# FFN input products in two token halves of 256 columns, with the activations moved by 320 bytes

## The chip, the core and the metric

The kernel runs on one core of a Trainium2 chip. The metric is the device time of one execution in microseconds, the median of several runs. The engines are PE (TensorE, matmuls, with its weight loads listed apart as PEld), DVE (VectorE), ACT (ScalarE), POOL (GpSimd) and SP (which here issues DMAs).

## The reference

One decoder layer for 512 tokens of width 1024 in float32. What matters here is its last part:

```
h = layer_norm(ALPHA * h + mixed @ w_out, ln1_g, ln1_b)
a, u = split(h @ w_ffn_in, 2)            # 1024 -> 2 x 2816
a = causal_dwconv(a, conv_w, conv_b)     # width 3, along the tokens
f = (gelu(a) * u) @ w_ffn_out            # 2816 -> 1024
out = layer_norm(ALPHA * h + f, ln2_g, ln2_b)
```

Ahead of it stand an input projection, a block-sparse attention branch, a pooling branch and their gated merge; the change does not touch them.

## The kernel before, in words

Every large product is made of three matmuls in a rounded 32-bit format (`fp32r`): both operands are split into a high part and a low part, and high x high, high x low and low x high are summed in PSUM. `mm3` (L144 to L148) issues the three; so nearly all matmuls of the profile stand on the lines L146, L147 and L148, and are told apart by the tile that they write (`fi` is the FFN input). A matmul holds one operand (128 x 128, loaded by LDWEIGHTS) and streams the other one past it, up to 512 columns.

The FFN input stage works feature-major. The activations after the first layer norm are transposed on PE (`ln1_T`, L537) into `hT_hi` and `hT_lo`, each 128 partitions x 8 k-tiles x 512 tokens of 4 bytes; a k-tile's row of 512 tokens is 2,048 bytes. They are the streamed operand. The weights `w_ffn_in` come in 44 chunks of 128 x 1024, gate and value columns alternating. `fetch` (L92) loads a chunk by a DMA on SP, ACT copies the high part (`whi`, L67) and DVE subtracts the low part (`wlo`, L68); there are three raw buffers and a ring of five split ones (`RING` = 5), and `weights(i)` (L139) asks for chunks up to three ahead. A buffer of the ring comes free when the last matmul that reads it is done.

`fi_mm(j, b, t)` (L575) computes chunk j for the tokens `t` into the PSUM bank `b`: 8 k-tiles x 3 matmuls. The first five chunks run in two passes of 256 tokens, the first 256 tokens of all five ahead of the others (L618 to L629), because the transposes of the last two token tiles (`ln1_T(2)` and `ln1_T(3)`) are still to be done in between. The other 39 chunks (L632 to L642) run with 512 columns at once. After every second chunk `gated` (L580) applies the convolution, GELU and the product with the value half on ACT and DVE, and `formed` (L607) prepares operands of the FFN output, which follows at L703 with products `foe`, `foa`, `fob`, `fod` and `fo_cut`.

The order on each engine is that of the program as a scheduler lays it out at build time. Tiles are placed in SBUF by pools in the order of their opening: `hTp` (L464) opens behind `ypool` and holds `hT_hi` and `hT_lo` alone, and the pool `fp` takes its place after the stage. With 16,384 bytes each, `hT_hi` begins at byte 101,056 of its partition and `hT_lo` at 117,440.

Of the kernel before, what the change touches and what calls it, by code (L numbers as in the profile page):

```python
# [8 lines left out]
F32 = mybir.dt.float32  # L9
# [5 lines left out]
P = 128  # L15
S = 512
D = 1024
KT = D // P
# [25 lines left out]
def layer_kernel(ctx: ExitStack, tc: tile.TileContext, xT, x, w_v, w_c, rel_bias, invcnt, w_group,  # L44
# [11 lines left out]
    def bank(name):  # L56
        return ps.tile([P, S], F32, tag="ps", name=name)
# [56 lines left out]
    def half(name, sl):  # L114
        return w_fo[int(name[1]) - 1, 2 - int(name[2])][:, sl]

    def piece(c):
        return slice(c * D, min((c + 1) * D, KH * S))
# [20 lines left out]
    def weights(i):  # L139
        while state["next"] <= min(i + LEAD, state["limit"]):  # L140
            fetch()
        return ready[i]

    def mm3(out_, w, a, start, stop, **kw):  # L144
        (wh, wl), (ah, al) = w, a
        nc.tensor.matmul(out_, wh, ah, start=start, stop=False, **kw)  # L146
        nc.tensor.matmul(out_, wh, al, start=False, stop=False, **kw)  # L147
        nc.tensor.matmul(out_, wl, ah, start=False, stop=stop, **kw)  # L148

    def split3(v, a):  # L150
        return tuple(t.rearrange("p (a c) -> p a c", a=a) for t in v)
# [83 lines left out]
    for kt in range(KT):  # L235
        wh, wl = split3(weights(kt // 2), 2)
        wh, wl = wh[:, kt % 2, :], wl[:, kt % 2, :]
# [189 lines left out]
    for f in range(KT):  # L427
        if f == KT - LEAD:
            state["limit"] = WO0 + RING - 1
        wh, wl = split3(weights(BR0 + f), KT)  # L430
# [4 lines left out]
        for br in (1, 0):  # L435
            b = bank(f"br{f}_{br}")
# [3 lines left out]
            t = bp.tile([P, S], F32, tag="m", name=f"m{f}_{br}", bufs=4)  # L440
# [21 lines left out]
    ytiles = [ypool.tile([P, S], F32, name=f"y{j}") for j in range(2)]  # L462
    hp = ExitStack()
    hTp = hp.enter_context(tc.tile_pool(name="hTp", bufs=1, reuse_waits="tile"))  # L464
    hT_hi = hTp.tile([P, KT, S], F32R, name="hT_hi")
    hT_lo = hTp.tile([P, KT, S], F32R, name="hT_lo")
    st = const.tile([P, NT, 4, 6], F32, name="st")
# [69 lines left out]
    def ln1_T(i):  # L537
        for n in range(2):
            b = bank(f"ht{i}_{n}")
            for k in range(4):  # L540
                kt = 4 * n + k
                nc.tensor.transpose(b[:, k * P:(k + 1) * P], xs[:, i, kt * P:(kt + 1) * P], ident)
            split(hT_hi[:, 4 * n:4 * n + 4, i * P:(i + 1) * P], hT_lo[:, 4 * n:4 * n + 4, i * P:(i + 1) * P],
                  b.rearrange("p (a c) -> p a c", a=4))
# [29 lines left out]

    def fi_mm(j, b, t):  # L575
        wh, wl = split3(weights(FI0 + j), KT)
        for kt in range(KT):
            mm3(b[:, t], (wh[:, kt, :], wl[:, kt, :]), (hT_hi[:, kt, t], hT_lo[:, kt, t]), kt == 0, kt == KT - 1)

    def gated(j, a, u):  # L580
        y = ytiles[j % 2]
        nc.scalar.activation(y, a, AF.Identity, bias=cvp[:, j, 3:4], scale=cvp[:, j, 2:3])
        nc.vector.scalar_tensor_tensor(y[:, 1:], a[:, :S - 1], cvp[:, j, 1:2], y[:, 1:], op0=ALU.mult, op1=ALU.add)
        nc.vector.scalar_tensor_tensor(y[:, 2:], a[:, :S - 2], cvp[:, j, 0:1], y[:, 2:], op0=ALU.mult, op1=ALU.add)  # L584
        nc.scalar.activation(y, y, AF.Gelu)  # L585
        nc.vector.tensor_tensor(fT[:, j, :], y, u, op=ALU.mult)  # L586
# [9 lines left out]
    t1, t2 = slice(0, 256), slice(256, 512)  # L596
# [10 lines left out]
    def formed(j):  # L607
        for c in cuts:
            if j == c.stop - 1:
                nc.vector.tensor_tensor(rd(c), side(0, c, t1), side(0, c, t2), op=ALU.subtract)  # L610
                side_split(0, c, rd(c))
            if j == KH + c.stop - 1:
                nc.vector.tensor_tensor(side(0, c, t2), side(1, c, t2), side(0, c, t2), op=ALU.subtract)
                nc.vector.scalar_tensor_tensor(rd(c), side(1, c, t2), -1.0, rd(c),
                                               op0=ALU.mult, op1=ALU.subtract)

    hb = {}
    for j in range(RING):  # L618
        hb[j] = bank(f"fi{j}")
        fi_mm(j, hb[j], slice(0, 256))  # L620
        if j == 0:
            ln1_T(2)
        elif j == RING - 2:
            ln1_T(3)
    for j in range(RING):
        state["limit"] = FI0 + RING + j
        fi_mm(j, hb[j], slice(256, 512))
        if j % 2:
            gated(j // 2, hb[j - 1], hb[j])  # L629
    state["limit"] = len(chunks) - 1  # L630
    ra = hw.tile([P, 8, 256], F32, tag="lnb", name="ra")
    for j in range(RING, 2 * NF):  # L632
        hb[j] = bank(f"fi{j}")
        fi_mm(j, hb[j], slice(0, S))
        if j % 2:
            f = j // 2
            gated(f, hb[j - 1], hb[j])
            formed(f)
            if f % 2 == 0 and f >= 6 and f < 6 + 2 * NC:
                c = f // 2 - 3  # L640
                nc.sync.dma_start(tw[:, piece(c)], half("B22", piece(c)))
                nc.gpsimd.dma_start(tw[:, piece(c)], half("B12", piece(c)), accum_op=ALU.add)  # L642
# [166 lines left out]
```

## Time and profile before

| what | value |
|---|---|
| median of 3 runs | 660.53 us (659.76 to 660.55) |
| the profiled execution: its own time | 659.63 us |
| its span, first to last instruction | 657.8 us |
| granted TensorE clock, mean | 0.996 |
| PE busy | 647.0 us |
| DVE / ACT / POOL busy | 384.9 / 284.7 / 95.5 us |

The profile is taken from one execution; the 1.8 us between its time and its span lie ahead of the first and behind the last instruction. Its views used here are: the page with the busy time of each engine and the chain of work that ended last; the groups of instructions by line, engine and shape, with count, total and mean; the timeline, one row for each instruction with its start and its length in us; the stretches, with the busy time of each engine in each; and the waits, which name the engine that waited, for whom, for how long in total, how often, and the longest. A matmul's end in the records is modelled, and matmuls overlap; what one costs in a gapless row is the distance from its start to the next one's.

### The profile page before, as it was taken

The page shows a single profiled execution, that of the slowest core. Times are in us where ns is not written, and L with a number is a line of the kernel's source. Part 1 is how long each engine was busy: PE and PEld are TensorE (multiplying, and loading weights), DVE is VectorE, ACT ScalarE, POOL GpSimd, SP SyncE. Part 2 cuts the span into 40 slices and gives each one's busy share as a digit, 9 for nine tenths or more (in the row PEclk, how much of TensorE's full clock was granted, in tenths as well). Part 3 has the DMA queues.
Part 4 walks back from the last instruction along what each step waited for, and adds up shares of the span by engine and source line. Part 5 has one row for each costly group of instructions (what it writes and reads, how often), then busy time and mean ns, then how long its engine had stood idle before and what let it go on. Part 6 is the DMA issues. An engine that isn't in the chain of part 4 may idle for free.

```text
span 657.8 us, 8016 instructions
## 1 busy us (share of the span) xinstructions
PE 647.0 (98%) x3082; PEld 537.6 (82%) x3082; DVE 384.9 (59%) x560; ACT 284.7 (43%) x393; POOL 95.5 (15%) x139
## 2 busy tenths in 40 slices
PE   8999999999999999999999999999999999999994
PEld 6888787877888888889988888888888888888884
DVE  6466665554532675398455344444534548789596
ACT  6547547585422233132443333333333336555452
POOL 1615351111000124102100000000000001123302
PEclk9999999999999999999999999999999999999998
DMA  8643222212222228209942222232222334979905
GB/s 319 213 145 97 81 83 77 97 64 70 92 96 97 96 97 305 79 1 302 255 146 97 97 96 97 96 99 99 95 96 100 96 99 107 219 180 190 283 4 128
DMA packets 24918, 83.70 MB, mean 127 GB/s; under 512 B 3240, under 2 KB 3496, under 8 KB 24624
## 3 DMA queue, kind: packets, MB, share of 16 engines
q1 hardware_dynamic: 19024, 63.24, 27.6%
q0 software_dynamic: 5280, 18.90, 13.3%
q10 hardware_dynamic: 576, 1.05, 0.5%
q8 instruction: 24, 0.39, 0.2%
q14 instruction: 14, 0.11, 0.1%
HBM read 80.01 MB, written 3.17 MB: 126 GB/s over the span
## 4 chain that ended last, share of the span: by engine, by line
PE 94%; DVE 2%; POOL 2%; ACT 1%; DMA 1%; issue 0%; DVEq 0%; ACTq 0%; POOLq 0%
PE fi L148 12%; PE fi L147 12%; PE fi L146 12%; PE g L146 4%; PE g L148 4%; PE g L147 4%; PE v L247 3%; PE wo L147 2%; PE br L148 2%; PE br L147 2%; PE wo L148 2%; PE wo L146 2%; PE br L146 2%; PE fod L148 2%; PE foa L148 2%; PE foa L147 2%
## 5 line engine op out<-in xcount | busy, mean ns | idle before, releaser
L68 DVE TENSOR_TENSOR wlo<-wraw,whi 128x1024 fp32r<-128x1024 f32 (+1 forms) x105 | 134.6, 1286 | 116.0 <-ACT whi L67 114.2
L67 ACT ACTIVATE whi<-wraw 128x1024 fp32r<-128x1024 f32 (+1 forms) x104 | 108.8, 1048 | 183.7 <-PE fi L147 83.6
L147 PE MATMUL fi<-hT_lo,whi 128*128 128x512 f32 (+1 forms) x392 | 143.8, 367 | 0.0
L148 PE MATMUL fi<-hT_hi,wlo 128*128 128x512 f32 (+1 forms) x392 | 143.8, 367 | 0.0
L146 PE MATMUL fi<-hT_hi,whi 128*128 128x512 f32 (+1 forms) x392 | 143.5, 368 | 0.0
L147 PEld LDWEIGHTS fi<-hT_lo,whi 128*128 128x128 f32 x392 | 73.9, 189 | 12.2
L148 PEld LDWEIGHTS fi<-hT_hi,wlo 128*128 128x128 f32 x392 | 73.9, 189 | 12.1
L146 PEld LDWEIGHTS fi<-hT_hi,whi 128*128 128x128 f32 x392 | 73.6, 189 | 12.1
L134 POOL DMA_DIRECT2D tw<-in_w_fo x18 | 15.8, 913 | 267.2 <-DVE wlo L68 267.2
L146 PE MATMUL g<-xT_hi,whi 128*128 128x512 f32 x128 | 50.3, 393 | 0.0
L148 PE MATMUL g<-xT_hi,wlo 128*128 128x512 f32 x128 | 49.9, 390 | 0.0
L147 PE MATMUL g<-xT_lo,whi 128*128 128x512 f32 x128 | 49.8, 389 | 0.0
L67 ACT ACTIVATE whi<-tw 128x1024 fp32r<-128x1024 f32 (+1 forms) x30 | 29.5, 985 | 25.0 <-PE fi L147 11.3
L586 DVE TENSOR_TENSOR fT<-y,fi 128x512 f32<-128x512 f32 x22 | 15.1, 688 | 40.3 <-PE fi L148 39.6
L68 DVE TENSOR_TENSOR wlo<-tw,whi 128x1024 fp32r<-128x1024 f32 (+1 forms) x30 | 33.4, 1131 | 8.4 <-ACT whi L67 8.3
L585 ACT ACTIVATE y<-y 128x512 f32<-128x512 f32 x22 | 13.9, 633 | 43.1 <-DVE y L584 43.1
L148 PEld LDWEIGHTS g<-xT_hi,wlo 128*128 128x128 f32 x128 | 24.0, 188 | 5.1
L146 PEld LDWEIGHTS g<-xT_hi,whi 128*128 128x128 f32 x128 | 24.0, 188 | 5.0 <-issue 0.2
L147 PEld LDWEIGHTS g<-xT_lo,whi 128*128 128x128 f32 x128 | 24.1, 188 | 4.9
L352 POOL TENSOR_SCALAR pp<-pp,rs 128x128 f32<-128x128 f32 (+3 forms) x32 | 21.8, 698 | 37.5 <-PE g L148 18.3
L444 POOL TENSOR_TENSOR mt<-m,m 128x512 f32<-128x512 f32 x8 | 11.2, 1394 | 96.0 <-DVE m L441 79.3
L146 PE MATMUL wo<-whi,mx_hi 128*128 128x512 f32 x64 | 25.0, 390 | 0.0
(204 smaller groups left out, 1185.6 us busy)
## 6 DMA issues: line engine op xcount, KB each, us to landing
wraw<-in_w_fi SPq DMA_DIRECT2D x44, 512.0 KB, 3.3
wraw<-in_w_c SPq DMA_DIRECT2D x28, 512.0 KB, 3.3
tw<-in_w_fo POOLq DMA_DIRECT2D x20, 512.0 KB, 7.3
tw<-in_w_fo SPq DMA_DIRECT2D x10, 512.0 KB, 3.6
wraw<-in_w_fo SPq DMA_DIRECT2D x10, 512.0 KB, 3.5
wraw<-in_w_br SPq DMA_DIRECT2D x8, 512.0 KB, 3.2
wraw<-in_w_out SPq DMA_DIRECT2D x8, 512.0 KB, 3.2
strip<-F_d POOLq DMA_DIRECT2D x8, 256.0 KB, 3.6
```

Source lines behind the costliest of these rows:

```text
L67: nc.scalar.activation(hi, src, AF.Copy)
L68: nc.vector.tensor_tensor(lo, src, hi.bitcast(F32), op=ALU.subtract)
L134: nc.gpsimd.dma_start(raw, half(then[1:], sl), accum_op=ALU.add)
L146: nc.tensor.matmul(out_, wh, ah, start=start, stop=False, **kw)
L147: nc.tensor.matmul(out_, wh, al, start=False, stop=False, **kw)
L148: nc.tensor.matmul(out_, wl, ah, start=False, stop=stop, **kw)
L247: nc.tensor.matmul(bs[j], xs_[j][a], (wh, wl)[b], start=kt == 0 and n == 0, stop=False)
L352: nc.gpsimd.tensor_scalar(pp[:, offs[i]:offs[i] + n], pp[:, offs[i]:offs[i] + n], rs[:, i:i + 1], 1.0, op0=ALU.mult, op1=ALU.mult)
L444: nc.gpsimd.tensor_tensor(mt, m[1], m[0], op=ALU.add)
L585: nc.scalar.activation(y, y, AF.Gelu)
L586: nc.vector.tensor_tensor(fT[:, j, :], y, u, op=ALU.mult)
```

## The change

An unused tile of 80 floats (320 bytes in each partition) is placed ahead of `hT_hi` in its pool, so that `hT_hi` begins at byte 101,376 and `hT_lo` at 117,760. `fi_mm` takes a tuple of token ranges and runs all k-tiles for one range after the other; the first five chunks pass one range of 256 tokens at a time, as before, and the 39 others pass both, so that each 512-column matmul becomes two of 256 columns with a weight load each. `t1` and `t2` are the slices 0:256 and 256:512 (L596).

```
+    hTp.tile([P, 80], F32, name="hT_gap")
     hT_hi = hTp.tile([P, KT, S], F32R, name="hT_hi")
     hT_lo = hTp.tile([P, KT, S], F32R, name="hT_lo")
...
     def fi_mm(j, b, t):
         wh, wl = split3(weights(FI0 + j), KT)
-        for kt in range(KT):
-            mm3(b[:, t], (wh[:, kt, :], wl[:, kt, :]), (hT_hi[:, kt, t], hT_lo[:, kt, t]), kt == 0, kt == KT - 1)
+        for c in t:
+            for kt in range(KT):
+                mm3(b[:, c], (wh[:, kt, :], wl[:, kt, :]), (hT_hi[:, kt, c], hT_lo[:, kt, c]), kt == 0, kt == KT - 1)
...
     for j in range(RING):
         hb[j] = bank(f"fi{j}")
-        fi_mm(j, hb[j], slice(0, 256))
+        fi_mm(j, hb[j], (t1,))
...
     for j in range(RING):
         state["limit"] = FI0 + RING + j
-        fi_mm(j, hb[j], slice(256, 512))
+        fi_mm(j, hb[j], (t2,))
...
     for j in range(RING, 2 * NF):
         hb[j] = bank(f"fi{j}")
-        fi_mm(j, hb[j], slice(0, S))
+        fi_mm(j, hb[j], (t1, t2))
```

More of the change, by code (lines that the diff above doesn't have):

```diff
@@ L464, in layer_kernel @@
     hTp = hp.enter_context(tc.tile_pool(name="hTp", bufs=1, reuse_waits="tile"))
+    hTp.tile([P, 80], F32, name="hT_gap")
     hT_hi = hTp.tile([P, KT, S], F32R, name="hT_hi")
@@ L576, in fi_mm @@
         wh, wl = split3(weights(FI0 + j), KT)
-        for kt in range(KT):
-            mm3(b[:, t], (wh[:, kt, :], wl[:, kt, :]), (hT_hi[:, kt, t], hT_lo[:, kt, t]), kt == 0, kt == KT - 1)
+        for c in t:
+            for kt in range(KT):
+                mm3(b[:, c], (wh[:, kt, :], wl[:, kt, :]), (hT_hi[:, kt, c], hT_lo[:, kt, c]), kt == 0, kt == KT - 1)
     def gated(j, a, u):
@@ L619, in layer_kernel @@
         hb[j] = bank(f"fi{j}")
-        fi_mm(j, hb[j], slice(0, 256))
+        fi_mm(j, hb[j], (t1,))
         if j == 0:
@@ L626, in layer_kernel @@
         state["limit"] = FI0 + RING + j
-        fi_mm(j, hb[j], slice(256, 512))
+        fi_mm(j, hb[j], (t2,))
         if j % 2:
@@ L633, in layer_kernel @@
         hb[j] = bank(f"fi{j}")
-        fi_mm(j, hb[j], slice(0, S))
+        fi_mm(j, hb[j], (t1, t2))
         if j % 2:
```

## The prediction

> **What bounds the kernel now.** I read the page's head first, then the stretches of the kernel, then the matmuls one by one.
>
> ```profile
> span 657.8 us, 8016 instructions
> PE 647.0 (98%) x3082; PEld 537.6 (82%) x3082; DVE 384.9 (59%) x560; ACT 284.7 (43%) x393; POOL 95.5 (15%) x139
> PE 94%; DVE 2%; POOL 2%; ACT 1%; DMA 1%; issue 0%; DVEq 0%; ACTq 0%; POOLq 0%
> ```
>
> PE is busy for 98% of the span, and 94% of the chain that ended last is PE's. A busy row is not yet a bound, because matmuls overlap; so the next view is the busy time of each engine in the stretches before the FFN input, in its first part (halves of 256 columns), in its main part (512 columns) and behind it.
>
> ```profile
> 301.20:331.50 30.30, 30.30 (x256) 30.28 (x255) 17.14 (x29) 10.87 (x15) 5.34 (x6) 1.00 1.00 287
> 331.50:543.90 212.40, 212.40 (x940) 175.97 (x939) 101.63 (x110) 70.93 (x85) 0.00 (x0) 1.00 0.29 100
> ```
>
> The columns are length, then PE, PEld, DVE, ACT, POOL busy with counts, the granted clock, DMA share and GB/s. In the main part PE has no idle time in 212.4 us, while DVE works 102 us and ACT 71 us. The clock is 1.00 in both. What this stage costs is therefore the number of matmuls times the distance from one start to the next. The grouped view, shapes apart, gives the counts:
>
> ```profile
> L146 PE MATMUL fi<-hT_hi,whi 128*128 128x512 f32 x312 | 121.4, 389 | 0.0
> L146 PE MATMUL fi<-hT_hi,whi 128*128 128x256 f32 x80 | 22.1, 285 | 0.0
> ```
>
> The same counts stand on L147 and L148, so 936 matmuls of 512 columns and 240 of 256. Their means (389 and 285 ns) are from start to modelled end, and they overlap; the price of one is the distance of starts, read from the timeline. Two stretches of it, the first with 512-column and 256-column forms next to each other:
>
> ```profile
> 300.99 0.39 PE L148 MATMUL wo<-whi,mx_lo 128*128 128x512 f32 x1
> 301.22 0.28 PE L146 MATMUL fi<-hT_hi,whi 128*128 128x256 f32 x1
> 301.33 0.28 PE L147 MATMUL fi<-hT_lo,whi 128*128 128x256 f32 x1
> 301.45 0.28 PE L148 MATMUL fi<-hT_hi,wlo 128*128 128x256 f32 x1
> ...
> 303.97 0.28 PE L148 MATMUL fi<-hT_hi,wlo 128*128 128x256 f32 x1
> ```
>
> ```profile
> 331.74 0.40 PE L146 MATMUL fi<-hT_hi,whi 128*128 128x512 f32 x1
> 331.97 0.40 PE L147 MATMUL fi<-hT_lo,whi 128*128 128x512 f32 x1
> ...
> 543.70 0.39 PE L148 MATMUL fi<-hT_hi,wlo 128*128 128x512 f32 x1
> 543.92 0.39 PE L146 MATMUL foe<-whi,sd_hi 128*128 128x512 f32 x1
> ```
>
> From 331.74 to 543.70 there are 935 steps: 211.96 us / 935 = **226.7 ns for 512 columns**. From 301.33 to 303.97 there are 22 steps: 2.64 us / 22 = **120.0 ns for 256 columns**. The difference, 106.7 ns for 256 columns, is 0.4167 ns for each column; so 512 columns take 213.3 ns and a rest of **13.3 ns** is left, and 256 columns take 106.7 ns with the same rest of 13.3 ns. In these two rows the rest does not depend on the length: it is paid for each matmul.
>
> **The change part by part.**
>
> *Two halves in place of one.* The main part has 44 - 5 = 39 chunks of weights, each with 8 k-tiles and 3 products: 936 matmuls, as counted above. Each becomes two of 256 columns, with its own weight load: PE has 936 matmuls and 936 loads more. By the rows, a pair costs 2 x 120.0 = 240.0 ns in place of 226.7, that is +13.3 ns; 936 x 13.3 ns = **+12.5 us**. All of it is on the path, since PE has no idle time here. A chunk's 24 products grow from 5.44 to 5.76 us.
>
> *The loads of weights.* The weight-load rows say whether they still hide:
>
> ```profile
> 305.08 0.19 PEld L148 LDWEIGHTS fi<-hT_hi,wlo 128*128 128x128 f32 x1
> 305.20 0.19 PEld L146 LDWEIGHTS fi<-hT_hi,whi 128*128 128x128 f32 x1
> 305.32 0.19 PEld L147 LDWEIGHTS fi<-hT_lo,whi 128*128 128x128 f32 x1
> ```
>
> In the halves they follow each other each 120 ns too, 0.19 us long, so two are in flight, and PEld is busy for 30.28 of 30.30 us against 175.97 of 212.40 in the main part. Their cost is inside the 120.0 ns, which I therefore don't add to. PE's stream of instructions doubles in rate, but the 240 matmuls of the halves already run at that rate for 30 us without a gap.
>
> *The order inside a chunk.* All k-tiles of the first half now come before those of the second. The last matmul of a chunk still ends both halves of the bank, so the gating on ACT and DVE, the ring of five weight buffers and the next stage are released by the same instruction as before. In the built programs the lists of ACT, DVE, POOL and SP, waits included, are the same; only PE's differs, by the 936. What waits in the main part waits for PE:
>
> ```profile
> ACT whi L67 <- PE fi L147: 95.0, 39, 4.4
> DVE fT L586 <- PE fi L148: 37.6, 19, 2.3
> SPq L108 <- DVE wlo L68: 159.2, 33, 7.2
> ...
> L68 DVE TENSOR_TENSOR wlo<-wraw,whi 128x1024 fp32r<-128x1024 f32 x36 | 44.1, 1224 | 63.4 <-ACT whi L67 62.2
> L67 ACT ACTIVATE whi<-wraw 128x1024 fp32r<-128x1024 f32 x36 | 38.3, 1063 | 85.9 <-PE fi L147 83.6 <-DMA wraw<-in_w_fi 2.3
> ```
>
> ACT waits 39 times for PE, to be given a buffer back, 95.0 us in total: weights are ready ahead, and a slower PE gives these engines more room. I cost this at nothing; the cover would be gone only with chunks shorter than the 2.29 us of copy and subtraction (1,063 and 1,224 ns), far below 5.4 us. Behind the stage, the FFN output begins one step after the last input matmul (543.70, 543.92) and moves as a whole.
>
> *The 320 bytes.* The empty tile has no instruction. Its only effect is the address of the activations: as the pools lay them out, hT_hi begins at byte 101,056 of its partition before (98 x 1024 + 704) and at 101,376 = 99 x 1024 after, hT_lo 16,384 further on; each half of a row (1,024 bytes) then begins on a multiple of 1,024. The weights, at 704 bytes past such a multiple plus steps of 512, don't move. What the address is worth no row shows: in this kernel every operand of this number type that PE streams begins 64 bytes past a multiple of 128 (704 or 960 past one of 1,024), and the distance is 226.7 ns in the input projections, the branch and output products and the FFN alike. I bound it from both sides. The best case is that the whole rest of 13.3 ns goes in all 2 x 936 + 240 = 2112 matmuls of the stage: 2112 x 13.3 = -28.2 us, against the +12.5. The worst, by the same size with the other sign, is +28.2 us. I take 0: a constant cost for each matmul needs no further cause to explain both rows.
>
> By the Trainium skill, page "SBUF — State Buffer", section Specifications, the memory has lines of 16 bytes, and a crossing into a new one is what costs. By that the edit is worth nothing, for 101,056 and 101,376 are both multiples of 16, and the forecast stays at +12.5 us; no run here shows it.
>
> The sum is made against the profiled execution, 659.63 us (span 657.8): 659.6 + 12.5 = 672.1. The median of the runs shown, 660.53, stands 0.9 above it, and I give a value between the two bases: **672.6 us**.
>
> **The rivals.**
>
> *The rest of 13.3 ns is a matter of the address (ends faster).* If PE fetches its stream in lines of 128 bytes, 32 columns of 4 bytes each, then 2,048 bytes that begin 64 past a line touch 17 lines and 1,024 bytes touch 9: 17 x 32 x 0.4167 = 226.7 ns and 9 x 32 x 0.4167 = 120.0 ns. That fits both rows as well as the constant does. At the new address it would be 8 lines, 106.7 ns: a pair 213.3 in place of 226.7 (936 x -13.3 = -12.5 us), and the 240 of the first part 13.3 ns less each (-3.2): 659.6 - 15.7 = 643.9. Against it: a load of weights goes with each matmul, its address is unchanged, and PEld is gapless in the halves, so a load may set the 120.0 ns there by itself; then nothing is won. The one shorter step of that part is the first (301.22 to 301.33, 0.11 us), whose load had been done under a long matmul. So the gain may stop at some 113 ns, where a pair costs 226 (936 x -0.7 = -0.6, 240 x -7 = -1.7: 657.3 us). The rival decides for faster wherever the new distance is under 114.1 ns (2112 x d = 936 x 226.7 + 240 x 120.0). Its time: between 643.9 and 657.3, at 109.5 ns, in the middle, 659.6 - 2112 x 4.6 ns = 649.9 us.
>
> The Trainium skill, page "TensorE: Matmul & The Clock Gate", section Back-to-back issue gap, gives columns / 2.4 + 2.5 ns for one warm matmul. By it a split would cost an estimated 936 x 2.5 = 2.3 us; at the old address the trace disagrees (120.0 ns against 109.2), and at the new one 109.2 ns would give an estimated -10.4 us. Its section on LDWEIGHTS gives columns / 1.2, 107 ns for 128, which would let the rival have nearly all of its gain.
>
> *The two nearly cancel (no change).* The distance falls to 113.5 to 114.7 ns: within 1.3 us of before, by the same equation.
>
> *The new address is worse.* The stream and the weights now begin at different places within 128 bytes (0 and 64), where before both were at 64. If that costs up to another 13.3 ns each, the time is up to 672.1 + 28.2 = 700.3. For it speaks only that no such pair is in the trace.
>
> **How the numbers follow.** A measurement of this kernel tells about 0.2% (1.3 us) from no change. Forecast, 671.5 to 673.5: 0.54. Slower, but with part of the rest gone (662 to 671): 0.04. Slower still: 0.02. Rival with the address: 0.35. Cancelled: 0.05. So slower 0.60, same 0.05, faster 0.35. The likeliest case's own range is 671.5 to 673.5; the range that is to hold 8 in 10 must reach into the faster rival, most of whose room lies above 646, so it goes from 646 to 674.
>
> **What would show it.** In the changed profile, the fi group of 512 columns is gone and that of 256 counts 2112. Distance of starts at 120.0 ns: the stage from 331.7 lasts 936 x 240.0 = 224.6 us in place of 212.2, and the first part stays at 30.5 us; the forecast holds. At 107 to 113 ns in both parts: the address mattered, and the first part, which is not split, would shrink by 1.7 to 3.2 us; this alone tells address from split. Above 120 ns: the new address is bad. The forecast would also be wrong if ACT or DVE became late, which would show as PE idle time before L146.

## The result and the profile after

The changed kernel takes 667.78 us (median of 4 runs, 667.68 to 669.95) against 660.54 us (4 runs, 659.76 to 660.57): ratio 1.012, 95% interval 1.0099 to 1.0142. It is slower by 7.2 us. The forecast was 672.6 us and slower, that is 12.1 us over this median of before (12.5 by its sum). The sign holds; the size came out smaller.

The head of the changed kernel's page, and its chain:

```profile
span 668.2 us, 9888 instructions
PE 657.4 (98%) x4018; PEld 583.5 (87%) x4018; DVE 385.0 (58%) x560; ACT 283.9 (42%) x393; POOL 93.1 (14%) x139
PE 93%; DVE 2%; POOL 2%; ACT 1%; DMA 0%; issue 0%; DVEq 0%; ACTq 0%; POOLq 0%
```

PE has 936 instructions and 936 weight loads more, DVE, ACT and POOL have as many as before, and the chain is still PE's. The stretches, with the columns as in the prediction, cut near the borders of the stage's parts (the first row begins 2.4 us ahead of the first FFN matmul, so it still holds some matmuls of the product before):

```profile
301.20:333.60 32.40, 32.40 (x268) 31.97 (x267) 19.07 (x31) 11.78 (x15) 5.33 (x6) 1.00 1.00 286
333.60:554.08 220.48, 220.48 (x1874) 220.48 (x1873) 101.64 (x110) 70.94 (x84) 0.00 (x0) 1.00 0.30 97
```

PE is gapless, the clock is 1.00, and in the main part PEld is now gapless too (220.48 of 220.48 us). The waits behind PE in the main part grew with it, as they should where PE sets the pace:

```profile
ACT whi L67 <- PE fi L147: 102.2, 38, 4.6
DVE fT L588 <- PE fi L148: 39.4, 19, 2.4
```

So again only the distance of starts counts. The groups and the timeline of the changed kernel, from the first matmul of the stage over the first of its main part to the first behind it:

```profile
L146 PE MATMUL fi<-hT_hi,whi 128*128 128x256 f32 x704 | 196.0, 279 | 0.0
```

```profile
303.58 0.28 PE L146 MATMUL fi<-hT_hi,whi 128*128 128x256 f32 x1
...
333.61 0.28 PE L146 MATMUL fi<-hT_hi,whi 128*128 128x256 f32 x1
...
553.97 0.28 PE L148 MATMUL fi<-hT_hi,wlo 128*128 128x256 f32 x1
554.09 0.39 PE L146 MATMUL foe<-whi,sd_hi 128*128 128x512 f32 x1
```

The main part takes 554.09 - 333.61 = 220.48 us for 1872 matmuls, **117.8 ns each** and not 120.0; a pair is 235.6 ns against 226.7. That is 936 x 8.9 ns = +8.3 us (220.48 against 212.19). The first part, which is not split, takes 30.0 us against 30.5: its 240 matmuls became about 2 ns shorter too. The sum is +7.8 us, and the medians say +7.2. This one profiled execution (669.95 us) is about 2.2 us above the other three of the kernel. In its trace the first FFN matmul starts 2.4 us later than in the trace of before (303.58 against 301.22), and the lag is there already at the first matmul of the input projections (29.18 against 26.74), ahead of everything that the change touches; the other three left no trace, so that this is their whole difference is likely and not shown.

The address was thus worth something, which I had put at nothing. The question for the experiments is what.

### The profile page after: what moved, and what is told of

It reads as the page before. It is cut to its first block, busy times and chain, and to the rows that moved or that the text cites. A ratio compares the mean times of both kernels' runs of the same rounds, so it can differ in the third digit from the quotient of the medians.

```text
span 668.2 us, 9888 instructions
## 1 busy us (share of the span) xinstructions
PE 657.4 (98%) x4018; PEld 583.5 (87%) x4018; DVE 385.0 (58%) x560; ACT 283.9 (42%) x393; POOL 93.1 (14%) x139
## 4 chain that ended last, share of the span: by engine, by line
PE 93%; DVE 2%; POOL 2%; ACT 1%; DMA 0%; issue 0%; DVEq 0%; ACTq 0%; POOLq 0%
PE fi L147 13%; PE fi L146 12%; PE fi L148 12%; PE g L146 4%; PE g L148 4%; PE g L147 4%; PE v L247 3%; PE wo L148 2%; PE br L148 2%; PE br L146 2%; PE wo L146 2%; PE wo L147 2%; PE br L147 2%; PE fod L147 2%; PE fod L146 1%; PE foa L147 1%
## 5 line engine op out<-in xcount | busy, mean ns | idle before, releaser
L147 PE MATMUL fi<-hT_lo,whi 128*128 128x256 f32 x704 | 196.9, 280 | 0.0
L148 PE MATMUL fi<-hT_hi,wlo 128*128 128x256 f32 x704 | 196.3, 279 | 0.0
L146 PE MATMUL fi<-hT_hi,whi 128*128 128x256 f32 x704 | 196.0, 279 | 0.0
L147 PEld LDWEIGHTS fi<-hT_lo,whi 128*128 128x128 f32 x704 | 132.2, 188 | 0.0
L146 PEld LDWEIGHTS fi<-hT_hi,whi 128*128 128x128 f32 x704 | 132.0, 188 | 0.0
L148 PEld LDWEIGHTS fi<-hT_hi,wlo 128*128 128x128 f32 x704 | 131.7, 187 | 0.0
L146 PE MATMUL g<-xT_hi,whi 128*128 128x512 f32 x128 | 50.3, 393 | 0.0
L148 PE MATMUL g<-xT_hi,wlo 128*128 128x512 f32 x128 | 49.9, 390 | 0.0
L147 PE MATMUL g<-xT_lo,whi 128*128 128x512 f32 x128 | 49.8, 389 | 0.0
L68 DVE TENSOR_TENSOR wlo<-tw,whi 128x1024 fp32r<-128x1024 f32 (+1 forms) x30 | 33.3, 1129 | 9.0 <-ACT whi L67 9.0
L148 PEld LDWEIGHTS g<-xT_hi,wlo 128*128 128x128 f32 x128 | 24.0, 188 | 5.1
L146 PEld LDWEIGHTS g<-xT_hi,whi 128*128 128x128 f32 x128 | 24.0, 188 | 5.0 <-issue 0.2
L147 PEld LDWEIGHTS g<-xT_lo,whi 128*128 128x128 f32 x128 | 24.0, 188 | 4.9
L146 PE MATMUL wo<-whi,mx_hi 128*128 128x512 f32 x64 | 25.0, 390 | 0.0
L148 PE MATMUL wo<-whi,mx_lo 128*128 128x512 f32 x64 | 24.9, 389 | 0.0
```

The source lines that it names most:

```text
L68: nc.vector.tensor_tensor(lo, src, hi.bitcast(F32), op=ALU.subtract)
```

## The experiments

All times are medians beside runs of the kernel before on the same chip (660.2 to 660.5 us); the distances of starts are from the traces. My theory was that PE fetches its stream in lines of 128 bytes, and that weight loads then set a floor of 117.8 ns. The rival was a small gain from the address for any matmul.

**The 320 bytes alone** (39 chunks at 512 columns):

```
+    hTp.tile([P, 80], F32, name="hT_gap")
     hT_hi = hTp.tile([P, KT, S], F32R, name="hT_hi")
```

> The kernel before with the empty 320 bytes alone; the 39 chunks stay at 512 columns. Line theory (a matmul streams its operand in lines of 128 bytes, so a start 64 bytes past a line costs one line, 13.3 ns; the 117.8 ns of the split kernel is then a floor set by the weight loads): 512 columns fall from 226.7 to between 213.3 and 216 ns, 936 x -13.3 to -10.7 ns, and the 240 short ones to 117.8 (-0.5 us): 647.5 to 650.0 us. Rival, small-address theory (the rest of 13.3 ns is constant, and the address takes 2.25 ns off each matmul of either length): 936 x -2.25 and 240 x -2.25 ns, 657.9 us.

Measured: 661.97 us, ratio 1.0024 (1.0014 to 1.0034). Both theories fall: it is slower. The timeline of this kernel, its first FFN matmul, the borders of the main part and four matmuls inside it:

```profile
301.83 0.28 PE L146 MATMUL fi<-hT_hi,whi 128*128 128x256 f32 x1
...
331.86 0.40 PE L146 MATMUL fi<-hT_hi,whi 128*128 128x512 f32 x1
...
399.85 0.39 PE L146 MATMUL fi<-hT_hi,whi 128*128 128x512 f32 x1
400.08 0.39 PE L147 MATMUL fi<-hT_lo,whi 128*128 128x512 f32 x1
400.31 0.39 PE L148 MATMUL fi<-hT_hi,wlo 128*128 128x512 f32 x1
400.54 0.39 PE L146 MATMUL fi<-hT_hi,whi 128*128 128x512 f32 x1
...
546.11 0.40 PE L146 MATMUL foe<-whi,sd_hi 128*128 128x512 f32 x1
```

214.25 us / 936 = **228.9 ns**: 2.2 ns more for 512 columns, at the same address that takes 2.2 ns off 256 columns (the first part, 301.83 to 331.86, is 30.0 us here too).

**The split alone**:

```
-    hTp.tile([P, 80], F32, name="hT_gap")
```

(taken out of the changed kernel)

> The split alone, activations at the old address. Both theories: 240.0 ns for a pair in place of 226.7, 936 x 13.3 ns = +12.5 us: 673.0 us. If it comes out at 667.8 as with the gap, the long run of short matmuls and not the address made 117.8 ns of 120.0.

Measured: 672.26 us, ratio 1.0175 (1.0158 to 1.0192). The timeline, borders of the main part:

```profile
331.60 0.28 PE L146 MATMUL fi<-hT_hi,whi 128*128 128x256 f32 x1
...
556.24 0.40 PE L146 MATMUL foe<-whi,sd_hi 128*128 128x512 f32 x1
```

224.64 us / 1872 = 120.0 ns. The split costs what the prediction worked out, +12.45 us in the trace; the 117.8 ns is the address's doing.

**64 bytes in place of 320** (`hTp.tile([P, 16], F32, name="hT_gap")`, unsplit):

> The kernel before with an empty 64 bytes in place of 320, unsplit: the activations begin on a multiple of 128 and 256 bytes, 768 past one of 1024. Line theory: as with 320 bytes, 647.5 to 650.0 us. Small-address theory: 657.9 if a multiple of 128 is enough, 660.5 if it needs a multiple of 512 or 1024.

Measured: 662.28 us, ratio 1.0024 (1.0014 to 1.0034), with 228.9 ns and a first part of 30.0 us. The same as 320 bytes: a start on a multiple of 1,024 is not what counts.

**The weights moved along** (one empty tile ahead of the weight pool moves everything behind it, the activations included):

```
+    const.tile([P, 80], F32, name="gap")
     wp = ctx.enter_context(tc.tile_pool(name="wp", bufs=1))
```

> The 320 bytes laid ahead of the weight buffers, so that weights and activations both begin on multiples of 1024; unsplit. The split weights are streamed in the token-major products (v 96, attention-and-merge output 192, FFN output 429 of 512 columns and 66 of 256). Line theory: the FFN input as with the gap alone, and 783 matmuls more of up to -13.3 ns (-10.4 us): 637 to 641 us. Small-address theory: (1176 + 783) x -2.25 ns = -4.4, 656.1 us. If what matters is that streamed and held operand begin at different places within 128 bytes, nothing changes: 660.5 us.

Measured: 664.65 us, ratio 1.0052 (1.0037 to 1.0067). The rows of this kernel: the FFN input's main part, then 42 steps of the gate projections ahead of it:

```profile
336.36 0.40 PE L147 MATMUL fi<-hT_hi,whi 128*128 128x512 f32 x1
...
548.55 0.39 PE L147 MATMUL foe<-whi,sd_hi 128*128 128x512 f32 x1
```

```profile
195.62 0.39 PE L147 MATMUL g<-xT_hi,whi 128*128 128x512 f32 x1
...
205.43 0.39 PE L147 MATMUL g<-xT_hi,whi 128*128 128x512 f32 x1
```

The FFN input is back at 212.19 / 936 = 226.7 ns, though its activations lie where they lay in the run with the gap alone: **not the address of the stream counts, but its place relative to that of the weights**. And the gate projections, whose stream stayed while the weights moved, went from 226.7 to 9.81 us / 42 = 233.6 ns (233.3 over the 214 steps without a gap around them). With 672 such matmuls in the input projections (28 tiles x 24), 672 x 6.6 ns = 4.4 us is the most that they can lose; from the starts of their matmuls they lose about 3.3 us, since not all of them stood in gapless rows. The output product ahead of the FFN (0.4 us) and the FFN output (0.5 us) make up the rest of the 4.2 us by which the median lies above before.

The FFN output tells the same with the roles exchanged: there the weights stream and the activations are held. Its product `fob` has in this run all its streamed starts 64 bytes behind the held ones, counted within 256:

```profile
578.62 0.39 PE L147 MATMUL fob<-whi,sd_hi 128*128 128x512 f32 x1
...
593.50 0.39 PE L149 MATMUL fob<-whi,sd_lo 128*128 128x512 f32 x1
```

14.88 us / 65 = 228.9 ns, the figure of the FFN input with the gap alone; before, the same 65 steps took 226.7 ns each.

Compare the two cases of a stream that lies elsewhere than the weights: the FFN input with the gap alone (228.9 ns) and the gate projections here (233.3 ns). Taken within 128 bytes, they are the same pair of places exchanged; within 256 bytes the streamed start lies 64 behind the weights in the first and 192 in the second. The next runs ask for the period.

**32 and 96 bytes, and the weights at the other place** (gap tiles of 8 and of 24 floats; `const.tile([P, 16], ...)` with a gap of 16):

> The kernel before with an empty 32 bytes ahead of the activations, unsplit: streamed starts 96 past a multiple of 128, weights still at 64. Relation theory (what counts is where the streamed start lies to the start of the weights within 128 bytes; equal gives 226.7 and 120.0 ns for 512 and 256 columns, streamed 0 and weights 64 gives 228.9 and 117.8, streamed 64 and weights 0 gives 233): a new distance, 512 columns between 226.7 and 233 ns, 660.5 to 666.4 us. Rival, granules of 64 bytes (only the 64-byte block of the start counts): 96 is in the block of 64, nothing changes, 660.5 us.

> The kernel before with an empty 96 bytes, unsplit: streamed starts 32 past a multiple of 128, weights at 64. Relation theory: a distance other than that at 0, 512 columns between 224 and 233 ns, 658 to 666 us. Granules of 64 bytes: 32 is in the block of 0, 228.9 and 117.8 ns as with 64 or 320 bytes, 662.1 us.

> 64 bytes ahead of the weight buffers and 64 more ahead of the activations, unsplit: weights at 0 and activations at 64 past a multiple of 128, the reverse of the changed kernel. Relation theory: 512 columns at 233 ns as in the input projections of the run with the weights alone moved against their stream, 256 columns other than 117.8 by the same sum; the other stages as in that run (664.7), the FFN input 936 x 6.3 ns more: 670.5 us. Rival, the streamed address alone counts: the FFN input is back at 226.7 and 120.0 ns, 664.7 us.

Measured: 665.85 us (ratio 1.0084, 1.0064 to 1.0104), 666.62 us (1.0086, 1.0053 to 1.0119) and 665.57 us (1.0075, 1.0055 to 1.0095). The main part is 218.40 us in the first two, 233.3 ns for a matmul, and 214.25 us in the third, 228.9 ns. Blocks of 64 bytes are out. The third kernel's borders of the main part:

```profile
337.76 0.40 PE L147 MATMUL fi<-hT_hi,whi 128*128 128x512 f32 x1
...
552.01 0.39 PE L147 MATMUL foe<-whi,sd_hi 128*128 128x512 f32 x1
```

In the third I had counted within 128 bytes and expected 233; within 256 the stream lies 64 behind the weights, as in the run with the gap alone, and takes the same 228.9.

**128, 192 and 224 bytes**, gap tiles of 32, 48 and 56 floats:

> The kernel before with an empty 128 bytes, unsplit: the streamed starts lie 128 bytes behind those of the weights, counted within 256. If the relation repeats every 128 bytes, this is the same as no gap: 226.7 and 120.0 ns, 660.5 us. Rival, it repeats every 256 (so the input projections, 192 apart after the weights alone were moved, take 233.2 ns, and the FFN input, 64 apart, 228.9): a distance not yet seen, above 226.7 ns for 512 columns, 661 to 667 us.

> The kernel before with an empty 192 bytes, unsplit. If the relation repeats every 256 bytes, the FFN input takes the 233.2 ns that the input projections took when 192 bytes lay between their two starts: 936 x 6.5 ns = +6.1 us, 666.6 us. Rival, it repeats every 128 bytes: as with 64 or 320 bytes, 228.9 ns, 662.1 us.

> The kernel before with an empty 224 bytes, unsplit. If the relation repeats every 128 bytes, this is the case of 96 bytes: 233.3 and 119.7 ns, 666.6 us. Rival, every 256 bytes: a place not yet seen, between 226.7 and 237 ns for 512 columns, 660.5 to 670 us; below 226.7 only if some place other than 0 is the best one.

Measured: 666.04 us (ratio 1.0094, 1.0074 to 1.0113), 666.06 us (1.0088, 1.0068 to 1.0108) and 666.88 us (1.0100, 1.0076 to 1.0124). The kernel with 128 bytes, borders of its main part:

```profile
331.76 0.40 PE L146 MATMUL fi<-hT_hi,whi 128*128 128x512 f32 x1
...
550.16 0.39 PE L146 MATMUL foe<-whi,sd_hi 128*128 128x512 f32 x1
```

218.40 us / 936 = 233.3 ns; the other two have the same. The period is not 128 bytes, and the 192 bytes foretold from the gate projections came out.

**256 bytes**, a gap tile of 64 floats:

> The kernel before with an empty 256 bytes, unsplit. If only the distance of the two starts within 256 bytes counts, the move is none: 226.7 and 120.0 ns, 660.2 us as before. Rival, any move away from the old place costs, or the relation has a longer period: 228.9 to 233.3 ns for 512 columns, 662 to 666.5 us.

Measured: 660.39 us, ratio 1.0005 (0.9992 to 1.0018): no change, by a move of 256 bytes. Its main part:

```profile
333.85 0.40 PE L146 MATMUL fi<-hT_hi,whi 128*128 128x512 f32 x1
...
546.04 0.39 PE L146 MATMUL foe<-whi,sd_hi 128*128 128x512 f32 x1
```

212.19 us / 936 = 226.7 ns. At the two places tried both ways, 0 and 64 (a gap of 64 and one of 320 bytes), the relation repeats every 256 bytes. In one table, for the FFN input. The 512 columns are the main part divided by 936. The 256 columns are the mean of the 236 steps without a gap in the first part; at 0 it is the main part of the split alone, and the first parts there give 119.9:

| streamed start behind the weights' start, within 256 bytes | 512 columns | 256 columns |
|---|---|---|
| 0 (before, split alone, both moved, gap 256) | 226.7 ns | 120.0 ns |
| 32 | 233.3 | 116.7 |
| 64 (the change, gap 64, gap 320, weights at 0) | 228.9 | 117.8 |
| 96 | 233.3 | 120.0 |
| 128 | 233.3 | 118.8 |
| 192 | 233.3 | 117.8 |
| 224 | 233.3 | 118.3 |

**Half a load.** Does the weight load take part, or only the two addresses?

```
-            mm3(b[:, t], (wh[:, kt, :], wl[:, kt, :]), (hT_hi[:, kt, t], hT_lo[:, kt, t]), kt == 0, kt == KT - 1)
+            nc.tensor.matmul(b[:, t], wh[:, kt, :], hT_hi[:, kt, t], start=kt == 0, stop=False)
+            nc.tensor.matmul(b[:64, t], wh[:, kt, :64], hT_lo[:, kt, t], start=False, stop=False)
+            nc.tensor.matmul(b[:, t], wl[:, kt, :], hT_hi[:, kt, t], start=False, stop=kt == KT - 1)
```

> The kernel before, but the second of the three products of the FFN input (high weights x low activations) holds only 64 of the 128 weight columns, so half of that small correction is left out and that load is half as long. If the rest of 13.3 ns comes from the reads of the load (128 columns of it against the stream), it halves for one matmul in three, whichever the length: 392 x -6.7 ns = -2.6 us, 657.9 us. If the rest belongs to the matmul itself or to the change of weights, nothing changes: 660.5 us.

Measured: 662.20 us, ratio 1.0024 (1.0012 to 1.0035). The loads of this kernel, and the borders of its main part:

```profile
399.98 0.14 PEld L579 LDWEIGHTS fi<-hT_lo,whi 128*64 128x64 f32 x1
400.22 0.19 PEld L580 LDWEIGHTS fi<-hT_hi,wlo 128*128 128x128 f32 x1
400.45 0.19 PEld L578 LDWEIGHTS fi<-hT_hi,whi 128*128 128x128 f32 x1
```

```profile
331.74 0.39 PE L578 MATMUL fi<-hT_hi,whi 128*128 128x512 f32 x1
...
546.82 0.39 PE L146 MATMUL foe<-whi,sd_hi 128*128 128x512 f32 x1
```

Neither number came: with the same addresses and streams, one shorter load in three (0.14 us in place of 0.19) moves the 512-column distance up, 215.08 us / 936 = 229.8 ns, and the 256-column one down, to 116.9 ns. That the load takes part in what a matmul costs, the runs with the weights moved had shown by its address. This run adds that it is not so many reads that are simply added. Whether the load's length does it is not shown: with 64 weight columns the matmul also writes 64 partitions in place of 128, and the run can't tell the two apart.

## Why the prediction was right in sign and off in size

- *PE's distances of starts bound the stage, and what waits, waits for PE.* Held: no idle time on PE before or after, nothing late behind it.
- *The split costs 936 x 13.3 ns = +12.5 us.* Held, shown alone: 120.0 ns, +12.45 us in the trace, +11.8 us in the medians.
- *The loads are inside the 120.0 ns, the new order in a chunk costs nothing.* Held for the sum.
- *The 320 bytes: "I take 0".* This is the term of the sum that was mis-sized. It is worth 2112 matmuls x -2.2 ns = -4.7 us in the split kernel, inside the bounds of -28.2 to +28.2. The reason I gave for 0, a constant cost for each matmul, is false: the rest depends on where the streamed start lies relative to the weights' start within 256 bytes. In the kernel before, all pairs that I had compared lay at the same place, 0, which is why one constant fitted them. I had set the two addresses against each other only in the last rival, within 128 bytes and for a loss alone.
- *The rival of the 128-byte lines* was right that the address matters and had the mechanism wrong: as run later, it foretold a gain for 512 columns too, which lose 2.2 ns. Its test, a first part that shrinks by 1.7 to 3.2 us, showed 0.5 us. Its point of decision, 114.1 ns, was sound: 117.8 lies above it, and the change is slower.
- *The rival "the new address is worse"*, from streamed and held operand at different places: it named the right relation with the wrong sign. The changed kernel's matmuls have 256 columns, and they gain 2.2 ns; 512 columns, which it no longer has there, lose 2.2 ns at this place and up to 6.6 at others.
- The 16-byte rule of the Trainium skill, page "SBUF — State Buffer", section Specifications, for which I said that no run shows it: by it the gap alone would be worth nothing. The runs disagree, 226.7 to 228.9 ns with a start that is a multiple of 16 both times.
- *The range.* The measured 667.78 us lies outside the 671.5 to 673.5 of the likeliest case. It is the case "slower, but with part of the rest gone (662 to 671)", which I gave a chance of 0.04. The range of 646 to 674 holds it because it was stretched down to a faster rival that did not come; that is luck. The sign is not: the split's +12.5 us is shown alone, and the address takes back well under half of it.

What is shown: the relation of the two starts, and its period of 256 bytes for the places tried. That reads of the load and reads of the stream get into each other's way in the memory is the explanation that fits, and it is argued, not shown. Against it stands the Trainium skill, page "TensorE: Matmul & The Clock Gate", section "Step-by-step: what each phase is for", by which the load has a read port of its own and takes no bandwidth from the running matmul. In the traces the load's address does change the distance of the matmuls (226.7 ns with both moved, 228.9 with one). Where load and stream would meet, no run here shows.

None of the kernels is faster than the one before. For 512 columns the place 0 is the best seen, and no pair of short matmuls of the FFN input is below its 226.7 ns (the least is 2 x 116.7).

## What to carry to other kernels

Price a split of matmuls by the distance of starts of the short form in the same kernel, not by its columns: here 256 columns cost 120.0 ns where half of 226.7 is 113.3. Where an edit moves an operand, compare its start with that of the operand that PE holds (here within 256 bytes), before calling the move free; a gap tile alone changed this kernel by about 6 us at the worse places. A constant that fits every row is no proof of its independence from something that is the same in every row.

## What the runs showed of the hardware that was not expected

Take 213.3 and 106.7 ns as the columns' own time; that is an estimate from the slope between the two rows at place 0. The rest beyond it, for three matmuls together (one turn of the product), then comes in steps for 512 columns: 40 ns at place 0, 46.7 at 64 and 60 at the five others. For 256 columns it is 40 at 0 and 96 and 33.3 at 64 and 192. These differ by multiples of 6.67 ns, by the same slope the time of 16 columns. The 256 columns at 32, 128 and 224 (30.1, 36.3 and 34.8 ns) and the run with half a load (49.4 for 512) don't fit such steps. Inside a turn the distances are unequal: with the gap alone most steps are 232, 226 and 229 ns from the starts on L146, L147 and L148, by the trace in whole nanoseconds.

The place doesn't settle the distance alone. In the run with the weights moved along, the 256-column matmuls of the FFN output lie at 64 like those of the changed FFN input, but their last 43 steps are shorter:

```profile
648.83 0.28 PE L148 MATMUL fo_cut<-wlo,sd_hi 128*128 128x256 f32 x1
...
653.70 0.28 PE L149 MATMUL fo_cut<-whi,sd_lo 128*128 128x256 f32 x1
```

4.87 us / 43 = 113.3 ns, against 117.8 ns. There, as in `fob`, the weights stream and the activations are held, with other steps between one start and the next. What makes this difference was not tried and stays open; it would make a pair some 226.6 ns, about the price of one matmul of 512 columns at place 0.
